# Two sums of weights per unit of seven products, made by GpSimd in place of VectorE

## The chip, the cores and the metric

The kernel runs on one core of one Trainium2 chip. The metric is the device time of one execution in microseconds (us); smaller is better. Five engines work beside each other, each through its own queue of instructions in order: TensorE (PE in the profile, with PEld for its weight loads), VectorE (DVE), ScalarE (ACT), GpSimd (POOL) and SyncE (SP, here only a queue that issues DMAs). An instruction waits in its queue until what it needs is there, and everything behind it in that queue waits too.

## The reference

One layer on 512 tokens of width 1024, all in fp32: a feed-forward block with half weight, a token mixer, a second feed-forward block with half weight, and a last norm.

```python
x = x + 0.5 * swiglu(rmsnorm(x, ffn1_norm), ffn1_w_gate, ffn1_w_up, ffn1_w_down)
x = x + token_mixer(rmsnorm(x, mix_norm), w_in, w_out, ...)
x = x + 0.5 * swiglu(rmsnorm(x, ffn2_norm), ffn2_w_gate, ffn2_w_up, ffn2_w_down)
return rmsnorm(x, final_norm)

def swiglu(x, w_gate, w_up, w_down):
    return (jax.nn.silu(x @ w_gate) * (x @ w_up)) @ w_down
```

The hidden width of a feed-forward block (FFN) is 2816, that is 22 tiles of 128. The change touches only the two FFNs.

## The kernel before

**Precision.** Activations lie transposed, as tiles of 128 features x 512 tokens. Each fp32 operand of a matmul is split into a high half (a copy rounded to the matmul's type fp32r, made by ScalarE) and a low half (what is left, a subtraction by VectorE). Each product is then three matmuls, high x high, high x low and low x high (`mm3`, lines 123 to 125 in the profile). For weights the high half is made in `high` (L391) and the low half in `low` (L395).

**Units of seven products.** The first gate and up tiles of an FFN are plain products. From tile 6 (first FFN) or tile 4 (second) on, the kernel works in units: two by two blocks of weights times two by two blocks of activations, done with seven block products in place of eight (Winograd's form of Strassen's method). A unit `("g", j)` makes the gates of the tiles j and j+1, `("u", j)` their ups, `("d", group, m)` adds a group of eight hidden tiles into the output tiles m and m+1. Plain products `("p", m)`, one for each output tile, stand between them. In order, an FFN has gate and up units, some plain products, four down units (group 0), gate and up units again, more plain products and four down units (group 1); the second FFN ends with half products `l` and `r`. There are 48 units in the two FFNs.

The seven products of a unit are listed in `SEVEN`, each with its block of weights, the PSUM bank it adds into and its block of activations:

```python
SEVEN = (("a11", "w", "b11"), ("s3", "z", "t3"), ("s2", "x", "t2"), ("a12", "w", "b21"),
         ("s1", "y", "t1"), ("a22", "x", "t4"), ("s4", "y", "b22"))
```

Each is 12 matmuls of 256 columns. Two banks are seeded: after product a11 ScalarE copies bank w into bank x (L420), and s2 adds onto it; after s2 it copies x into y, and s1 adds onto it. TensorE can't begin the seeded product before the copy.

**Sums of weights.** Four of the seven blocks of weights are sums. s1 and s3 are made by DMAs in `weight_sums`: SP loads a block into a slot (L346), then a DMA from GpSimd's queue adds a second block onto it (L347, an accumulating DMA, which waits for SP's to land). s2 and s4 are made by VectorE in `total`: s2 = s1 + the left half of the first row of weights (raw0), into a tile of its own (L373); s4 = raw0's right half + s2, in place (L375). So s4 waits until s2's high and low halves are made, and s2 waits for s1. The rows of weights come through `load` (L355) into a pool of three buffers, raw0 and raw1 of a unit in turn; raw1 of a unit therefore takes the buffer that raw0 of the unit before it had, whose last reader on VectorE is s4.

**Order.** Around the units the order on VectorE, ScalarE, SP and GpSimd is written out by a small planner (`pipeline`): every step has a nominal due time, counted from the nominal start of its product (`starts[t]`; STEP is one product of a unit, seven to a unit), and a rank; a heap hands the steps out in order of time, then rank, and each engine gets its instructions in that order. For product t of a unit the steps before the change are:

- `weight_sums`: 14 steps ahead of the unit's first product (two units); later where its slots are still in use by an earlier unit, namely two steps into that unit, and one step later than that rule for one unit of an FFN (`("g", PLAIN + 10)`)
- `load`: 7 steps ahead of the unit
- `total`: 5 steps ahead of product s2 or s4
- `high`: 4 steps ahead; `low`: 3 steps ahead
- `product` itself, and behind it the steps that take its result out of PSUM

The down units share two pairs of slots for s1 and s3 (`GROUP_SUMS`), which the first gate and up unit after group 0 use too, so there the later time applies. After an up unit the casts and subtractions that ready the gates for the down products (`kept`: L547 to L591, with L429 and L432 for the sums of activations) run on ScalarE and VectorE during the unit that follows.

Of the kernel before, what the change touches and what calls it, by code (L numbers as in the profile page):

```python
# [18 lines left out]
ALU = mybir.AluOpType  # L19
# [34 lines left out]
STEP, PLAIN_STEP, HALF_STEP = 1410, 4080, 2130  # L54
# [9 lines left out]
def tile_macaron(ctx: ExitStack, tc, xs, xT, wf, wgu1, wst1, wd1, wdg1, wqk, wv, wo, wgu2, wst2, wd2,  # L64
                 wdg2, lams, relb, onehot, addc, out):
    nc = tc.nc
    V, A, G, T = nc.vector, nc.scalar, nc.gpsimd, nc.tensor
# [136 lines left out]
    def ffn(wgu, wst, wd, wdg, n0, n1, norm, early, res, nm, hooks, ended, first=None,  # L204
# [77 lines left out]
        def up(j):  # L282

            wh, wl = up_w[j]
            pu = ups[j] = pp.tile([P, S], F32, tag="t", name=f"pu{nm}{j}", bufs=2)
            for k in range(KD):
                o = k // 2 * P + k % 2 * 4 * P
                o = slice(o, o + P)
                mm3(pu[:], wh[:, o], wl[:, o], xh[k][:], xl[k][:], k == 0, k == KD - 1)
                yield k  # L290

        def up_weights(j):
            up_w[j] = get_w(wst[j - n1][1], f"su{nm}{j}")
# [18 lines left out]
        ops, begin, starts, now = [], {}, [], 0  # L312
# [14 lines left out]
        def sum_slots(u):  # L327
            if u[0] == "d":
                return GROUP_SUMS[u[2] // 2 % 2]
            if u == units[0]:  # L330
                return PAIR_SLOTS[0][:2]
            if u[1] == PLAIN + 8:
                return GROUP_SUMS[u[0] == "u"]
            o = 2 if u[0] == "g" else 4
            return PAIR_SLOTS[(u[1] - PLAIN) // 2 % 4][o:o + 2]

        sums, raws, second, made, half, g, hs = {}, {}, {}, {}, [], {}, {}
# [29 lines left out]
        def total(t):  # L367

            u, o = ops[t]
            r0 = raws[u][0]  # L370
            if o[0] == "s2":
                s2 = second[u] = tp.tile([P, S], F32, tag="ob", name=f"s2{nm}{t}")[:]
                V.tensor_tensor(s2, sums[u][0][:], r0[:, :512], op=ALU.add)  # L373
            else:
                V.tensor_tensor(second[u], r0[:, 512:], second[u], op=ALU.add)  # L375

        def high(t):
            u, o = ops[t]
# [31 lines left out]
        def at(time, rank, f, *a):  # L410
            count[0] += 1
            heapq.heappush(events, (time, rank, count[0], f, a))
# [4 lines left out]
        def run(until):  # L417
            while events and events[0][0] <= until:
                _, _, _, f, a = heapq.heappop(events)
                f(*a)  # L420
# [210 lines left out]
        def pipeline():  # L631
            seen = {}
            for t, (u, o) in enumerate(ops):
                if o[0] in ("p", "l"):
                    at(starts[t] - 2 * PLAIN_STEP, 1, load, u)
                    at(starts[t] - 3 * STEP, 3, high, t)
                    at(starts[t] - 2 * STEP, 2.5, low, t)
                elif o[0] != "r":
                    if t == begin[u]:
                        if u != units[0]:  # L640

                            time, s0 = starts[t] - 14 * STEP, sum_slots(u)
                            if s0 in seen:
                                time = max(time, starts[begin[seen[s0]] + 2])
                            seen[s0] = u
                            if u == ("g", PLAIN + 10):


                                time += STEP
                            at(time, 1, weight_sums, u)  # L650
                        at(starts[t] - 7 * STEP, 1.5, load, u)
                    if o[0] in ("s2", "s4"):
                        at(starts[t] - 5 * STEP, 2, total, t)
                    at(starts[t] - 4 * STEP, 3, high, t)
                    at(starts[t] - 3 * STEP, 2.5, low, t)
                at(starts[t], 4, product, t)
            if bias is not None:
                at(starts[begin["p", plain]], 5, bias[0])
                at(starts[begin["d", 1, 0] + 2], 5, bias[1])
            up_weights(n1 + 1)  # L660
            for i in range(2):
                for k in up(n1 + i):
                    prepared(n1 + i, k)
                    run((8 * i + k - 15) * 680)
            run(1 << 40)
# [10 lines left out]
        def prepared(j, k):  # L676
            if (j, k) in prepare:
                f, p = prepare[j, k]
                f(p)

        order = ExitStack()
        for j in range(j0, n1):
# [9 lines left out]
            for hf in range(2):  # L692
                wh, wl = get_w(wgu[j, hf], f"gu{nm}{j}_{hf}")
                for kk in range(4):
                    k = hf * 4 + kk
                    for c, pt in ((0, pg), (1, pu)):
                        o = kk * 256 + c * P
# [14 lines left out]
        with order, tc.manual_schedule(engines={mybir.EngineType.DVE, mybir.EngineType.Activation}):  # L712
            pipeline()
# [20 lines left out]
    with tc.manual_schedule(engines={mybir.EngineType.DVE, mybir.EngineType.Activation}):  # L734
        for t in range(4):
            raw = wp.tile([P, 1024], F32, tag="raw", name=f"raw_f{t}")
            h, l = w_place()
            for kk in range(2):
# [18 lines left out]
                for j in range(2):  # L757
                    for c in range(2):
                        o = kk * 512 + (2 * j + c) * P
# [99 lines left out]
    at = {}  # L859
# [611 lines left out]
```

## Time and profile before

| what | value |
|---|---|
| time, median of 3 runs | 936.92 us (936.84 to 937.58) |
| the profiled execution's own time | 937.02 us |
| its span in the trace | 935.3 us |
| TensorE busy | 924.3 us, 99% of the span |
| VectorE busy | 728.5 us, 78% |
| ScalarE busy | 543.4 us, 58% |
| GpSimd busy | 98.2 us, 11% |
| DMA, over the span | 136.71 MB, 146 GB/s |

How to read it: a row of a timeline gives the start in us from the span's start, the duration in us, the engine, the line of the kernel, the operation, and what it writes and reads by the program's names (buffer numbers left out); at the end, in brackets, the idle time of the engine before it and what ended that. A name ends in a or b for the first or second FFN, and g, u, d, p in it stand for the kind of unit: `pxdb` is bank x of a down unit of the second FFN, `s2a` a sum s2 of the first. In a list of waits a row gives the engine, the line waiting, what released it, the time in total, how often, and the longest where that is given. In a view by line, the three numbers behind a count are the shortest, median and longest duration in ns. In the table of windows each row gives the stretch, its length, then the busy time and count of instructions for TensorE, its weight loads, VectorE, ScalarE and GpSimd, the granted clock, the share of the DMA engines and GB/s.

### The profile page before, as it was taken

To read this page: it belongs to the slowest core of one execution; us is meant where nothing else is said; L and a number is where in the kernel's file an instruction comes from. 1 tells how busy PE (TensorE), PEld (TensorE's weight loads), DVE (VectorE), ACT (ScalarE), POOL (GpSimd) and SP (SyncE) were. 2 spreads that over 40 slices of the span, in tenths; PEclk is the share of its full clock that TensorE was granted. 3 is DMA by queue.
4 is the path that set the end of the run, shared out by engine and by line. 5 is a ranking of instruction groups with operands and counts; after the bars stand their busy time and mean duration, and the time that the engine had idled before them with its cause. 6 is when DMAs were issued, how large, how long until landed. Compare 5 with 4: busy or idle time off the path is not lost.

```text
span 935.3 us, 17089 instructions
## 1 busy us (share of the span) xinstructions
PE 924.3 (99%) x6384; PEld 851.0 (91%) x6384; DVE 728.5 (78%) x1504; ACT 543.4 (58%) x1121; POOL 98.2 (11%) x117
## 2 busy tenths in 40 slices
PE   9999999999999999999999999999999999999996
PEld 7888999999999999988978778889999999999996
DVE  6797887677888897678876556797888777888785
ACT  7455664355664575566766664455666455665572
POOL 0001101112202100000000003110111012111000
PEclk9999999999999999999999999999999999999998
DMA  7456646578747562433343213454674677865542
GB/s 251 130 148 147 160 125 173 137 189 220 184 131 203 144 169 91 136 112 113 91 135 91 68 35 129 131 165 106 180 193 116 164 198 193 206 180 152 141 120 91
DMA packets 60372, 136.71 MB, mean 146 GB/s; under 512 B 6832, under 2 KB 9136, under 8 KB 60288
## 3 DMA queue, kind: packets, MB, share of 16 engines
q1 hardware_dynamic: 46288, 110.14, 36.0%
q0 software_dynamic: 14000, 25.47, 17.5%
q8 instruction: 50, 0.82, 0.4%
q14 instruction: 34, 0.28, 0.1%
HBM read 130.30 MB, written 2.14 MB: 142 GB/s over the span
## 4 chain that ended last, share of the span: by engine, by line
PE 94%; DVE 4%; issue 1%; ACT 1%; DMA 1%; SPq 0%; DVEq 0%
PE pv L922 2%; PE pv L921 2%; PE pv L920 2%; PE pwo L123 2%; PE pwo L124 2%; PE pwo L125 2%; PE pua L125 2%; PE pua L124 2%; PE pua L123 2%; PE pq L123 1%; PE pq L124 1%; PE pq L125 1%; PE pk L123 1%; PE pk L125 1%; PE pk L124 1%; PE pda L125 1%
## 5 line engine op out<-in xcount | busy, mean ns | idle before, releaser
L1041 ACT ACTIVATE pr<-pr,mx 128x128 f32<-128x128 f32 (+3 forms) x64 | 36.0, 563 | 35.0 <-DVE mx L1038 34.4
L1038 DVE CUSTOM_DVE_ANT_0 pr<-sc,strip 128x128 f32<-128x128 f32 (+3 forms) x64 | 30.7, 487 | 22.4 <-PE sc L1036 22.1
L391 ACT CAST w<-s2b 128x512 fp32r<-128x512 f32 x50 | 31.0, 620 | 17.1 <-DVE s2b L373 15.6
L395 DVE TENSOR_TENSOR w<-s2b,w 128x512 fp32r<-128x512 f32 x50 | 34.2, 685 | 7.3 <-ACT w L391 7.3
L391 ACT CAST w<-s2a 128x512 fp32r<-128x512 f32 x46 | 28.6, 621 | 18.6 <-DVE s2a L373 15.7
L150 POOL TENSOR_TENSOR sq<-sq,sqt 128x512 f32<-128x512 f32 x7 | 11.0, 1564 | 244.1 <-ACT sqt L149 244.0
L395 DVE TENSOR_TENSOR w<-s2a,w 128x512 fp32r<-128x512 f32 x46 | 31.5, 684 | 6.6 <-ACT w L391 6.5
L920 PE MATMUL pv<-w,xh 128*128 128x256 f32 x128 | 36.2, 283 | 0.0
L921 PE MATMUL pv<-w,xl 128*128 128x256 f32 x128 | 36.2, 283 | 0.0
L922 PE MATMUL pv<-w,xh 128*128 128x256 f32 x128 | 36.2, 283 | 0.0
L123 PE MATMUL pq<-xh,w 128*128 128x512 f32 x64 | 26.2, 410 | 0.0
L123 PE MATMUL pwo<-mh,w 128*128 128x512 f32 x64 | 25.6, 399 | 0.0
L124 PE MATMUL pq<-xl,w 128*128 128x512 f32 x64 | 25.1, 393 | 0.0
L125 PE MATMUL pq<-xh,w 128*128 128x512 f32 x64 | 25.1, 392 | 0.0
L125 PE MATMUL pk<-xh,w 128*128 128x512 f32 x64 | 25.0, 391 | 0.0
L123 PE MATMUL pk<-xh,w 128*128 128x512 f32 x64 | 25.0, 391 | 0.0
L124 PE MATMUL pk<-xl,w 128*128 128x512 f32 x64 | 25.0, 390 | 0.0
L124 PE MATMUL pwo<-ml,w 128*128 128x512 f32 x64 | 25.0, 390 | 0.0
L125 PE MATMUL pwo<-mh,w 128*128 128x512 f32 x64 | 25.0, 390 | 0.0
L921 PEld LDWEIGHTS pv<-w,xl 128*128 128x128 f32 x128 | 24.4, 191 | 0.3
L920 PEld LDWEIGHTS pv<-w,xh 128*128 128x128 f32 x128 | 24.4, 191 | 0.2
L922 PEld LDWEIGHTS pv<-w,xh 128*128 128x128 f32 x128 | 24.5, 191 | 0.0
(691 smaller groups left out, 3992.8 us busy)
## 6 DMA issues: line engine op xcount, KB each, us to landing
raw_qk<-wqk_dram SPq DMA_DIRECT2D x16, 512.0 KB, 3.4
raw0bg<-wst_dram SPq DMA_DIRECT2D x9, 512.0 KB, 4.9
raw_gua<-wgu_dram SPq DMA_DIRECT2D x8, 512.0 KB, 3.4
raw0ag<-wst_dram SPq DMA_DIRECT2D x8, 512.0 KB, 4.5
raw0ad<-wdg_dram SPq DMA_DIRECT2D x8, 512.0 KB, 5.3
strip<-bias_rows SPq DMA_DIRECT2D x16, 256.0 KB, 3.7
raw_v<-wv_dram SPq DMA_DIRECT2D x8, 512.0 KB, 3.3
raw_wo<-wo_dram SPq DMA_DIRECT2D x8, 512.0 KB, 3.3
```

The lines of the kernel that those rows point to most:

```text
L123: T.matmul(po, wh, mh, start=first, stop=False, skip_group_check=on)
L124: T.matmul(po, wh, ml, start=False, stop=False, skip_group_check=on)
L125: T.matmul(po, wl, mh, start=False, stop=last, skip_group_check=on)
L150: G.tensor_tensor(sq[:], sq[:], t[:], op=ALU.add)
L391: A.copy(made[t][0], source(t))
L395: V.tensor_tensor(l, source(t), h.bitcast(F32), op=ALU.subtract)
L920: T.matmul(po, xh[k][:, xs], wh[:, o:o + 256], start=k == 0, stop=False)
L921: T.matmul(po, xl[k][:, xs], wh[:, o:o + 256], start=False, stop=False)
L922: T.matmul(po, xh[k][:, xs], wl[:, o:o + 256], start=False, stop=k == KD - 1)
L1038: V.tensor_tensor_reduce(out=pi, in0=ps[:, :w], in1=st["b"][m][:, w - 1::-1], op0=ALU.add, op1=ALU.min, scale=1.0, scalar=3.0e38, accum_ou ...
L1041: A.activation(pi, pi, AF.Exp, scale=-1.0, bias=st["mx"][:, m, i:i + 1], accum_out=st["ls"][:, m, i:i + 1])
```

## The change

Both adds of `total` go from VectorE's queue (`V`) to GpSimd's (`G`), and their due times move: s2 from 5 steps ahead of its product to 6.5, s4 from 5 to 5.5. The due time sets the place in the order in which GpSimd's queue gets the adds among the accumulating DMAs of `weight_sums`. Nothing else is changed.

```diff
             if o[0] == "s2":
                 s2 = second[u] = tp.tile([P, S], F32, tag="ob", name=f"s2{nm}{t}")[:]
-                V.tensor_tensor(s2, sums[u][0][:], r0[:, :512], op=ALU.add)
+                G.tensor_tensor(s2, sums[u][0][:], r0[:, :512], op=ALU.add)
             else:
-                V.tensor_tensor(second[u], r0[:, 512:], second[u], op=ALU.add)
+                G.tensor_tensor(second[u], r0[:, 512:], second[u], op=ALU.add)
...
                     if o[0] in ("s2", "s4"):
-                        at(starts[t] - 5 * STEP, 2, total, t)
+                        at(starts[t] - (6 if o[0] == "s2" else 5) * STEP - STEP // 2, 2, total, t)
```

## The prediction

> **What bounds the kernel now.** I read the page first, then the list of waits of TensorE's two streams, then the table of windows.
>
> ```profile
> span 935.3 us, 17089 instructions
> ...
> PE 924.3 (99%) x6384; PEld 851.0 (91%) x6384; DVE 728.5 (78%) x1504; ACT 543.4 (58%) x1121; POOL 98.2 (11%) x117
> ```
> ```profile
> PEld pyga L123 <- DVE rbc_n L423: 0.4, 1, 0.4
> ...
> PEld pyda L123 <- DVE x L432: 0.3, 1, 0.3
> ```
> ```profile
> 800.00:820.00 20.00, 20.00 (x171) 20.00 (x171) 17.66 (x34) 12.76 (x27) 3.45 (x4) 1.00 0.85 226
> ```
>
> TensorE is busy for 99% of the span. In all the units of seven products it waited for another engine only where the two rows of the second fence say, 0.7 us together. The window is typical of units that make gates and ups: TensorE full, granted clock 1.00, VectorE 17.66 of 20 us. So work taken off VectorE can win at most those 0.7 us; what counts is whether the change brings TensorE to a stop.
>
> **What moves.** The view by line of the two adds:
>
> ```profile
> L373 DVEq EVENT_SEMAPHORE  x48: 21/21/21, 78.3 to 901.0; - x48
> ...
> L373 DVE TENSOR_TENSOR s2b<-s1bg,raw0bg x9: 679/681/685, 636.2 to 839.3; 128x512 f32<-128x512 f32 x9
> ```
>
> There are 48 units, each with one add for s2 and one for s4: 96 instructions of 0.68 us leave VectorE. In a row each takes 0.60 us of its time (below, 825.31 to 825.91), so VectorE is given 57.6 us. On the path that is worth nothing beyond the 0.7 us. No DMA is added. But GpSimd's queue, until now only descriptors in these stages, gets two waiting adds per unit, and the second load of a unit's rows (raw1) now waits on SP for GpSimd's s4, since it takes the buffer which s4 reads.
>
> **The price of an add on GpSimd** is seen where it adds squares, same shape and type:
>
> ```profile
> 563.56 1.34 POOL L150 TENSOR_TENSOR sq<-sq,sqt 128x512 f32<-128x512 f32 x1 [228.49 <-ACT sqt L149]
> 566.22 3.06 POOL L150 TENSOR_TENSOR sq<-sq,sqt 128x512 f32<-128x512 f32 x2 [1.32 <-ACT sqt L149]
> 572.46 1.29 POOL L150 TENSOR_TENSOR sq<-sq,sqt 128x512 f32<-128x512 f32 x1 [3.17 <-ACT sqt L149]
> 577.48 1.78 POOL L150 TENSOR_TENSOR sq<-sq,sqt 128x512 f32<-128x512 f32 x1 [3.73 <-ACT sqt L149]
> ```
> ```profile
> 564.48 0.69 DVE L1204 TENSOR_TENSOR x<-pwo,x 128x512 f32<-128x512 f32 x1
> ...
> 566.35 1.78 DVE L115 TENSOR_TENSOR w<-raw_wo,w 128x512 fp32r<-128x512 f32 x1
> 568.06 1.77 DVE L137 SCALAR_TENSOR_TENSOR elb<-x,x,ehb 128x512 fp32r<-128x512 f32 x1
> ...
> 577.37 0.74 DVE L137 SCALAR_TENSOR_TENSOR elb<-x,x,ehb 128x512 fp32r<-128x512 f32 x1
> ```
> ```profile
> 565.46 0.62 ACT L149 ACTIVATE sqt<-x 128x512 f32<-128x512 f32 x1
> ```
>
> Undisturbed it takes 1.29 us, and starts 0.14 us after what it waits for (565.46 + 0.62 to 566.22). The two engines exclude each other. VectorE's subtraction at 566.35 took 1.78 instead of 0.68: it went on only at 567.45, 1.23 us after GpSimd's start. GpSimd's add at 577.48 took 0.49 longer, because of VectorE's instruction that ended at 578.11: GpSimd got in 0.14 before that end. Back to back they alternate (GpSimd's pair of 3.06 us, VectorE's 1.78 and 1.77). VectorE's add at 564.48, with one input in PSUM, ran in 0.69 beside GpSimd: only instructions with two SBUF inputs are held. The subtractions that make the low halves (L395) and those on the gates (L429, L547) are of that kind.
>
> [...]
>
> **First term: a gate unit behind a pair** (timelines of VectorE, ScalarE and TensorE):
>
> ```profile
> 822.98 0.68 DVE L395 TENSOR_TENSOR w<-s2b,w 128x512 fp32r<-128x512 f32 x1
> 823.58 0.41 DVE L547 TENSOR_TENSOR h0b<-g0b,h0b 128x256 fp32r<-128x256 f32 x1
> ...
> 824.36 0.42 DVE L429 TENSOR_TENSOR g0b<-g0b 128x256 f32<-128x256 f32 x1
> 824.71 0.68 DVE L395 TENSOR_TENSOR w<-raw0bg,w 128x512 fp32r<-128x512 f32 x1
> 825.31 0.68 DVE L547 TENSOR_TENSOR h2b<-g1b,h1b 128x512 fp32r<-128x512 f32 x1
> 825.91 0.42 DVE L429 TENSOR_TENSOR g0b<-g1b,g0b 128x256 f32<-128x256 f32 x1
> ```
> ```profile
> 826.36 0.62 ACT L577 CAST h3b<-g0b 128x512 fp32r<-128x512 f32 x1 [0.64 <-DVE g0b L429]
> ...
> 827.67 0.38 ACT L420 COPY pygb<-pxgb 128x256 f32<-128x256 f32 x1
> ```
> ```profile
> 827.39 0.28 PE L123 MATMUL pwgb<-xh,w 128*128 128x256 f32 x1
> ...
> 828.81 0.28 PE L123 MATMUL pygb<-txb,w 128*128 128x256 f32 x1
> ```
>
> GpSimd's s4 overwrites s2, so it waits for the low half of s2: 823.66 + 0.14, and then for L547, till 823.85. VectorE's L429 is held to 825.08 and ends at 825.50. GpSimd's next add, s2 of the coming unit, has all it needs; it gets in at 825.36 and holds VectorE to 826.59. So the low half of 824.71 begins at 826.59, 1.88 us late, and so does the second L429 (the add at 826.24, gone from VectorE, stood only behind it). ScalarE's cast h3 waits for that L429, and behind the cast in ScalarE's queue stands the copy that seeds bank y. It now ends at 828.05 + 1.88 = 829.93; TensorE wants it at 828.81. Cover 0.76, stall 1.12 us. Next to be late would be the low half itself: it ends at 827.27, its product begins at 827.39 and reads it third, so that one just holds. The saved VectorE time then brings the up unit back on time. These casts:
>
> ```profile
> ACT h3a L577 <- DVE g0a L429: 9.0, 8, 2.3
> ...
> ACT h3b L577 <- DVE g0b L429: 8.9, 8, 2.3
> ```
>
> Of the 16, four fall into plain products, which have no seeded bank, and one behind the first, single gate; 11 x 1.12 = 12.3 us.
>
> **Second term: GpSimd's queue in the down units.** By the planner's times, the sums of weights (L346, L347) of a unit whose slots are shared are issued two steps into the unit two before it, and s2 of the unit in between two and a half steps into that: behind both accumulating DMAs, which wait for SP's loads to land. On VectorE s2 did not wait for them.
>
> ```profile
> 745.01 0.68 DVE L375 TENSOR_TENSOR s2b<-raw0bd,s2b 128x512 f32<-128x512 f32 x1
> ...
> 749.83 0.68 DVE L373 TENSOR_TENSOR s2b<-s1bd,raw0bd 128x512 f32<-128x512 f32 x1
> ...
> 755.29 0.69 DVE L395 TENSOR_TENSOR w<-s1bd,w 128x512 fp32r<-128x512 f32 x1
> ```
> ```profile
> 752.21 0.85 POOL L347 DMA_DIRECT2D s3bd<-wdg_dram  x1 [1.27 <-DMA s3bd<-wdg_dram]
> 761.51 0.86 POOL L347 DMA_DIRECT2D s1bd<-wdg_dram  x1 [8.45 <-DMA s3bd<-wdg_dram]
> 762.05 1.21 POOL L347 DMA_DIRECT2D s3bd<-wdg_dram  x1
> ```
> ```profile
> 756.00 0.33 SPq L346 DMA_DIRECT2D s1bd<-wdg_dram  x1
> ```
> ```profile
> 750.62 0.62 ACT L391 CAST w<-s2b 128x512 fp32r<-128x512 f32 x1 [1.14 <-DVE s2b L373]
> 751.15 0.61 ACT L391 CAST w<-raw0bd 128x512 fp32r<-128x512 f32 x1
> ...
> 755.17 0.36 ACT L420 COPY pxdb<-pwdb 128x256 f32<-128x256 f32 x1 [2.29 <-PE pwdb L125]
> ```
> ```profile
> 756.39 0.28 PE L123 MATMUL pxdb<-h5b,w 128*128 128x256 f32 x1
> ```
> ```profile
> 766.33 0.28 PE L123 MATMUL pxdb<-h5b,w 128*128 128x256 f32 x1
> ```
>
> A unit lasts 766.33 - 756.39 = 9.94 us. The queue closes a ring: s2 on GpSimd (1.29), its high half on ScalarE (0.11 later, as 749.83 to 750.62; 0.62), its low half (0.68), s4 on GpSimd (0.14, holds VectorE 1.23), two low halves (0.60, 0.68), SP's next load of sums (0.02, as 755.29 to 756.00), to the first accumulate 5.51 (756.00 to 761.51), both out 1.75 (761.51 to 762.05 + 1.21): 12.63 us, 2.69 longer than a unit. Before, the ring was open, since s2 was done at 750.51 without GpSimd.
>
> The first turn starts in the unit of 756.39. There GpSimd is free at 753.06, or 752.46 as the add of 745.01 no longer holds back the low half that SP waits for. s2 ends at 753.75; behind its high half stand two more (0.53 each, 750.62 to 751.15) and then the copy that seeds x: 755.45 to 755.81, in time. One turn on, s2 ends at 766.38 and the copy at 768.44, where TensorE wants 766.33: 2.1 us. The next two lose 2.7 each; the fourth some 2.5, as its sums have slots of their own and SP waits for one low half less. Such a run, 10.0 us, comes in each FFN with the first group of down units and the two units behind; the second group has only two such waits and GpSimd free about a microsecond earlier: I estimate 1 us each. Together 22 us.
>
> **Sum.** 937.0 (profiled, 0.1 above the median) + 12.3 + 22.0 - 0.7 = 970.6 us.
>
> **Rivals.** *Queue alone, 958.3.* VectorE, back to back, may keep GpSimd out until its run ends; then L429 is not late. The pair at 566 to 570 speaks against it, but shows one case. *Exclusion alone, 948.6.* The loads might land sooner when fewer are in flight, closing the gap of 2.69; 5.51 comes from one turn. *Nothing lost, 936.3*: both covers hold (0.76 for the copy to y, 0.58 for the first turn), as GpSimd's s2 runs well ahead in the pairs and VectorE, with 57.6 us less, catches up. It decides if VectorE's delay at L429 stays under 0.76 and a turn under 9.94. This is also the other side: the whole gain would be 0.7 us. *More stops, 994:* all 32 gate and up units lose 1.12, not 11; against it stands the up unit's spare time, for it VectorE idles 2.34 us in the 20 of the window.
>
> **How the numbers follow.** Both terms 0.55 (own range 958 to 984: each term a third smaller or 40% larger), queue alone 0.17, exclusion alone 0.12, nothing lost 0.08, more stops 0.08. The range, 947 to 986, leaves out the last two. Under 0.2% (1.9 us) a measurement of this kernel hardly tells from no change. Slower 0.92; within 0.2% 0.06 and faster 0.02, both from nothing lost.
>
> **What would show it.** GpSimd's busy time should rise by some 96 x 1.3 = 125 us or more, with adds of 1.3 to 1.9 us. VectorE's subtractions beside them should stretch to near 1.8. TensorE should wait for ScalarE's copies (L420) into y in gate units, about 1.1 us, and into x in units around the down groups, 2 to 3 us, three or four in a row, with s2 on GpSimd right behind an accumulate. If TensorE's waits for L420 are missing, or s2 starts before the accumulates, the prediction is wrong.

## The result, and the profile after

The changed kernel takes 968.9 us in the median of four runs (966.57 to 971.77). The kernel before took 937.1 us beside it, so the ratio is 1.034, with an interval of 1.0326 to 1.0353. The prediction said 970.6 us, in a range of 947 to 986. The profiled execution of after took 971.77 us, the longest of the four, with a span of 970.0: against the span before, 34.7 us more. Between the medians the rise is 31.8 us; the account below is of the profiled execution, how the other three divide is not known.

The page of after, with the busy times and, last, the shares of the chain of work that ended last:

```profile
span 970.0 us, 17117 instructions
...
PE 933.7 (96%) x6384; PEld 855.3 (88%) x6384; DVE 738.8 (76%) x1408; ACT 540.4 (56%) x1121; POOL 238.2 (25%) x213
...
PE 74%; DVE 11%; issue 5%; ACT 4%; POOL 3%; DMA 2%; SPq 0%; DVEq 0%; POOLq 0%; ACTq 0%
```

GpSimd's busy time has risen by 140.0 us for 96 adds. VectorE has 96 instructions fewer and yet is busy for 10.3 us more: it stands still inside its instructions (the subtraction at 834.68 below takes 1.77 us, the same one of before at 824.71 took 0.68). TensorE's share of the chain has fallen to 74%. Its list of waits in after (what it waited for: us in total, times, longest):

```profile
PE pyga L123 <- ACT pyga L420: 5.3, 6, 1.2
PE pygb L123 <- ACT pygb L420: 5.2, 6, 0.9
PE pxda L123 <- ACT pxda L420: 3.4, 4, 1.3
...
PE pxub L123 <- ACT pxub L420: 2.8, 1, 2.8
```

These are the two kinds of stop that the prediction named: for the copy that seeds bank y of the gate units (twelve, near 1 us), and for the copy that seeds bank x around the down groups.

**A gate unit of after**, from the timelines of GpSimd, VectorE, ScalarE and TensorE; its first product starts at 832.45:

```profile
833.07 1.40 POOL L375 TENSOR_TENSOR s2b<-raw0bg,s2b 128x512 f32<-128x512 f32 x1 [1.66 <-DVE w L395]
834.43 1.47 POOL L373 TENSOR_TENSOR s2b<-s1bu,raw0bu 128x512 f32<-128x512 f32 x1
```
```profile
833.69 1.06 DVE L429 TENSOR_TENSOR g0b<-g0b 128x256 f32<-128x256 f32 x1
834.68 1.77 DVE L395 TENSOR_TENSOR w<-raw0bg,w 128x512 fp32r<-128x512 f32 x1
...
836.98 0.42 DVE L429 TENSOR_TENSOR g0b<-g1b,g0b 128x256 f32<-128x256 f32 x1
```
```profile
837.42 0.62 ACT L577 CAST h3b<-g0b 128x512 fp32r<-128x512 f32 x1 [2.46 <-DVE g0b L429]
...
838.74 0.37 ACT L420 COPY pygb<-pxgb 128x256 f32<-128x256 f32 x1
```
```profile
839.16 0.38 PE L123 MATMUL pygb<-txb,w 128*128 128x256 f32 x1 [0.87 <-ACT pygb L420]
```

GpSimd stops VectorE twice (L429 takes 1.06 us and L395 1.77, where they took 0.42 and 0.68 before), and VectorE gets one instruction in between (L429 until 834.75). The second L429 starts 4.53 us into the unit. Before it did so at 825.91, 2.78 into the unit of 823.13; it is 1.75 late. Behind it stand the cast of h3 and the copy to y, which ends at 839.11; TensorE waits for it in the last row.

**A turn of the ring in after**: SP's loads, GpSimd and VectorE around a down unit that starts at 784.03.

```profile
778.60 0.33 SPq L346 DMA_DIRECT2D s1bd<-wdg_dram  x1
...
789.78 0.33 SPq L346 DMA_DIRECT2D s1bg<-wst_dram  x1
```
```profile
782.79 0.87 POOL L347 DMA_DIRECT2D s1bd<-wdg_dram  x1 [5.37 <-DVE w L395]
783.37 1.18 POOL L347 DMA_DIRECT2D s3bd<-wdg_dram  x1
783.94 1.93 POOL L373 TENSOR_TENSOR s2b<-s1bd,raw0bd 128x512 f32<-128x512 f32 x1
787.32 1.28 POOL L375 TENSOR_TENSOR s2b<-raw0bd,s2b 128x512 f32<-128x512 f32 x1 [1.46 <-DVE w L395]
```
```profile
786.55 0.69 DVE L395 TENSOR_TENSOR w<-s2b,w 128x512 fp32r<-128x512 f32 x1 [3.32 <-ACT w L391]
...
787.49 1.66 DVE L395 TENSOR_TENSOR w<-raw0bd,w 128x512 fp32r<-128x512 f32 x1
789.07 0.68 DVE L395 TENSOR_TENSOR w<-s1bd,w 128x512 fp32r<-128x512 f32 x1
```

s2 starts right behind the second accumulating DMA, and the next load of s1 waits for the low half that ends at 789.75. One turn, from load to load, is 789.78 - 778.60 = 11.18 us, longer than a unit of 9.94. The eight turns around the first groups of the two FFNs took 11.03 to 12.33 us, 11.5 in the mean.

Comparing the start of every product with its start before gives the loss of each unit, 34.7 us in all. The prediction's eleven gate units are the first two rows. The clock of the last row is told of at the end; the 1.5 us that each of its two falls cost are taken out of the rows above (the eleventh gate unit lost 3.96 in all).

| where | predicted, us | measured, us |
|---|---|---|
| ten gate units behind a pair, copy of y | 11.2 | 11.3 (1.11 to 1.14 each) |
| the eleventh (starts at 242.21) | 1.1 | 2.45 |
| first group of down units and behind, first FFN | 10.0 | 0.74 + 1.24 + 1.76 + 1.75 = 5.5 |
| the same, second FFN | 10.0 | 1.12 + 1.09 + 1.98 + 3.05 = 7.2 |
| second groups | 2.0 | 3.2 + 1.8 = 5.0 |
| gate unit that starts at 93.86, and the gain | -0.7 | 0.8 - 0.5 = 0.3 |
| clock at half rate, twice | 0 | 2.9 |

### The profile page after: what moved, and what is told of

It reads as the page before. It is cut to its first block, busy times and chain, and to the rows that moved or that the text cites. A ratio compares the mean times of both kernels' runs of the same rounds, so it can differ in the third digit from the quotient of the medians.

```text
span 970.0 us, 17117 instructions
## 1 busy us (share of the span) xinstructions
PE 933.7 (96%) x6384; PEld 855.3 (88%) x6384; DVE 738.8 (76%) x1408; ACT 540.4 (56%) x1121; POOL 238.2 (25%) x213
## 4 chain that ended last, share of the span: by engine, by line
PE 74%; DVE 11%; issue 5%; ACT 4%; POOL 3%; DMA 2%; SPq 0%; DVEq 0%; POOLq 0%; ACTq 0%
DVE w L395 4%; ACT w L391 2%; PE pv L922 2%; PE pv L921 2%; PE pv L920 2%; PE pwo L123 2%; PE pwo L124 2%; PE pwo L125 2%; PE pua L124 1%; PE pua L123 1%; PE pua L125 1%; PE pq L123 1%; PE pq L124 1%; PE pq L125 1%; PE pk L123 1%
## 5 line engine op out<-in xcount | busy, mean ns | idle before, releaser
L395 DVE TENSOR_TENSOR w<-s2b,w 128x512 fp32r<-128x512 f32 x50 | 34.2, 684 | 21.1 <-ACT w L391 21.1
L395 DVE TENSOR_TENSOR w<-s2a,w 128x512 fp32r<-128x512 f32 x46 | 31.4, 683 | 15.3 <-ACT w L391 15.3
L347 POOL DMA_DIRECT2D s1ag<-wst_dram x8 | 7.2, 898 | 84.0 <-DMA s3ag<-wst_dram 40.3
L920 PEld LDWEIGHTS pv<-w,xh 128*128 128x128 f32 x128 | 24.4, 191 | 0.2
```

The lines of the kernel that those rows point to most:

```text
L347: nc.gpsimd.dma_start(t[:], b, accum_op=ALU.add)
L395: V.tensor_tensor(l, source(t), h.bitcast(F32), op=ALU.subtract)
L920: T.matmul(po, xh[k][:, xs], wh[:, o:o + 256], start=k == 0, stop=False)
```

## The experiments

**order: the ring alone is opened.** From the changed kernel, the sums of weights come one product later into the unit whose slots they take over, and so stand behind s2 of the next unit in GpSimd's queue:

```diff
-                                time = max(time, starts[begin[seen[s0]] + 2])
+                                time = max(time, starts[begin[seen[s0]] + 3])
...
-                                time += STEP
+                                time += 3 * STEP
```

> The changed kernel, with the sums of weights by DMA handed out one step later where their slots are shared (and three steps later for the one unit that has a step of its own), so that s2 stands ahead of the accumulating DMAs in GpSimd's queue. Theory (two causes: a ring through GpSimd's queue in and behind the down units, and VectorE held at L429 in the gate units): TensorE's waits for the copies into bank x go, the waits for the copies into y stay at some 1.1 us each; 11 x 1.13 = 12.4 us over the kernel before, so 949 to 951. Rival one (the accumulating DMAs themselves are slower because GpSimd is busy, wherever they stand): waits for x stay, 965 to 970. Rival two (VectorE is held in general, order does not matter): 966 to 972.

Measured: 953.4 us (953.1 to 954.8), ratio 1.0173 (1.0156 to 1.019). The waits for x are gone; in TensorE's waits in order those for y remain:

```profile
PE pygb L123 <- ACT pygb L420: 5.6, 6, 1.2
```

So the place of s2 behind the accumulating DMAs makes the ring, and opening it gives back 15.5 us. The regular gate units still lose 1.13 us each. Two others lose 1.86 and 1.67, which is part of why the time is above what was expected.

**copy: the copy of y alone is given more time.** The cast of h3, behind which the copy stood in ScalarE's queue, is handed out a step later, so that it stands behind the copy:

```diff
-            put(n + 2 * STEP, t0_parts)
+            at(n + 3 * STEP, 1, t0_parts)
```

> The changed kernel, with the cast h3 handed out one step later, so that in ScalarE's queue it stands behind the copy that seeds bank y. VectorE and GpSimd exclude each other as before. Theory: the waits for copies into y go (11.3 us, and what the unit with 3.96 us lost that way), the waits for x stay: 955 to 959. Rival (VectorE's lost time itself holds TensorE, through the low halves): little changes, 966 to 970, with TensorE waiting for VectorE's L395 instead of ScalarE's L420.

Measured: 960.7 us (960.1 to 961.4), ratio 1.0248 (1.0233 to 1.0263), somewhat above the 955 to 959 expected. No wait for a copy into y is left, and the regular gate units lose 0.1 us each, ahead of their last product. The waits for x stay, this one first among TensorE's waits in copy:

```profile
PE pxda L123 <- ACT pxda L420: 3.6, 4, 1.2
```

The medians lie 8.2 us apart, the spans 970.0 - 959.4 = 10.6. In the spans the gate units give back 11.6 and one fall of the clock less 1.4, while the waits for x cost 2.4 more than in after.

**both: the two edits together.**

> Both edits together. Theory: the two causes are all there is, so 937 to 940, no faster than the kernel before by more than 0.7 us. If the causes feed each other or a third is there: 943 or more.

Measured: 942.25 us (941.0 to 942.6), ratio 1.0049 (1.0034 to 1.0064). No wait for L420 into x or y is left, so the two terms of the prediction are two separate losses. But the time is 2 to 5 us above what two causes alone should leave: the units still lose 4.7 us, 1.45 and 1.18 of it in two gate units, one in each FFN (the other ten gate units lose 0.12 each, three down units 0.9 together). In the second of these, GpSimd and VectorE of both did this:

```profile
806.44 1.10 POOL L347 DMA_DIRECT2D s3bg<-wst_dram  x1
807.00 1.86 POOL L375 TENSOR_TENSOR s2b<-raw0bg,s2b 128x512 f32<-128x512 f32 x1
808.25 1.85 POOL L373 TENSOR_TENSOR s2b<-s1bu,raw0bu 128x512 f32<-128x512 f32 x1
```
```profile
807.26 3.13 DVE L429 TENSOR_TENSOR g0b<-g0b 128x256 f32<-128x256 f32 x1
```

VectorE did not get in between the two adds; it was held through both. The same stands in after, in the eleventh gate unit of the table:

```profile
243.79 3.75 DVE L395 TENSOR_TENSOR w<-raw0ag,w 128x512 fp32r<-128x512 f32 x1
```

In both cases s4 comes about 0.6 us behind the issue of an accumulating DMA. In the kernel of both, VectorE is held through two adds in four of the 32 pairs that stand back to back, for 3.1 us or more; these are the four with a DMA issue 0.56 us ahead of s4. In the other 28 the last issue lies 0.84 us or more ahead, and none of VectorE's instructions beside them takes longer than 1.8. That is a third cause, tested below.

**s4_only: s2 goes back to VectorE at its old place, s4 stays on GpSimd.**

```diff
-                G.tensor_tensor(s2, sums[u][0][:], r0[:, :512], op=ALU.add)
+                V.tensor_tensor(s2, sums[u][0][:], r0[:, :512], op=ALU.add)
...
-                        at(starts[t] - (6 if o[0] == "s2" else 5) * STEP - STEP // 2, 2, total, t)
+                        at(starts[t] - 5 * STEP - (STEP // 2 if o[0] == "s4" else 0), 2, total, t)
```

> Only s4 on GpSimd, at its place in the changed kernel; s2 on VectorE at its place in the kernel before. Theory: no add on GpSimd stands behind an accumulating DMA that anything near waits for, so no ring; one stop of VectorE in the gate unit makes L429 some 0.7 us late, within the cover of 0.76, so 937 to 939. Rival (each add on GpSimd costs by its exclusion, half as many adds): half of the y waits, 942 to 944.

Measured: 938.7 us (938.2 to 940.3), ratio 1.0017 (1.0008 to 1.0026). Of the waits for L420 into x or y one of 0.3 us is left, in a gate unit that loses 0.7. The one add s4 per unit nearly fits under TensorE, but does not make the kernel faster; it costs 0.7 to 2.4 us.

**s2_only: the other half.** s2 stays on GpSimd at its new place, s4 goes back to VectorE.

```diff
-                G.tensor_tensor(second[u], r0[:, 512:], second[u], op=ALU.add)
+                V.tensor_tensor(second[u], r0[:, 512:], second[u], op=ALU.add)
...
-                        at(starts[t] - (6 if o[0] == "s2" else 5) * STEP - STEP // 2, 2, total, t)
+                        at(starts[t] - 5 * STEP - (STEP + STEP // 2 if o[0] == "s2" else 0), 2, total, t)
```

> The first sum s2 stays on GpSimd at its new place, the second sum s4 goes back to VectorE. Theory (the ring closes through s2 alone, as s2 stands behind the two accumulating DMAs of the next-but-one unit in GpSimd's queue): the ring stays, a turn is about 0.4 us shorter, since s4 costs a VectorE slot of about 0.6 us in place of a stop of 1.2; the waits of TensorE for the copies that seed x (L420) remain, some 15 us instead of 18 to 19. In gate units there is one stop of VectorE per unit, not two: 0 to 0.5 us each for the copy of y. 950 to 957 us. Rival (the ring needs s4 on GpSimd, which follows s2 in the same queue, or the loss of gate units comes from either add): without s4 the x waits go, 937 to 942.

Measured: 960.3 us (958.6 to 961.3), ratio 1.0245 (1.0229 to 1.026). The ring stands with s2 alone: the units around the down groups lose 17.7 us and the gate units 0.5 or less, 0.7 in one. That the loss would get smaller did not come true, and the time is above the 950 to 957 expected. SP's loads and GpSimd in s2_only:

```profile
769.43 0.33 SPq L346 DMA_DIRECT2D s1bd<-wdg_dram  x1
...
780.60 0.33 SPq L346 DMA_DIRECT2D s1bg<-wst_dram  x1
```
```profile
773.64 0.87 POOL L347 DMA_DIRECT2D s1bd<-wdg_dram  x1 [7.75 <-DVE w L395]
774.89 0.85 POOL L347 DMA_DIRECT2D s3bd<-wdg_dram  x1 [0.39 <-issue]
```

This turn is 11.17 us, as the one shown of after. What s4 saves is lost here between the two accumulating DMAs: the second starts 1.25 us behind the first, in after 0.58. In the mean of eight turns it is 11.3 us against 11.5, so 0.2 shorter where 0.4 was expected.

**order_twice: the price of one more stop.** The kernel of order, with the add that makes s2 issued twice (in the runs with added lines the line numbers are one or two higher):

```diff
                 G.tensor_tensor(s2, sums[u][0][:], r0[:, :512], op=ALU.add)
+                G.tensor_tensor(s2, sums[u][0][:], r0[:, :512], op=ALU.add)
```

> The kernel of the run order (no ring), with the add that makes s2 issued twice on GpSimd: the second one writes the same values again, so the output is the same and only GpSimd's and VectorE's time is added. Theory (VectorE is stopped for 1.23 us by each add of GpSimd, and in a gate unit nothing is left to cover it): a third stop ahead of the second L429 costs about 1.15 us more in each of the 11 gate units, L420 waits of about 2.3 instead of 1.2, about 966 us. Rival (VectorE's instruction gets in between the two adds and the low half is what was late, not a count of stops): 953 to 956, as in order.

Measured: 978.9 us (977.3 to 982.1), ratio 1.0451 (1.0428 to 1.0475). GpSimd in one gate unit, then VectorE:

```profile
289.67 1.41 POOL L376 TENSOR_TENSOR s2a<-raw0ag,s2a 128x512 f32<-128x512 f32 x1 [4.99 <-DVE w L396]
291.04 1.46 POOL L373 TENSOR_TENSOR s2a<-s1au,raw0au 128x512 f32<-128x512 f32 x1
292.58 1.62 POOL L374 TENSOR_TENSOR s2a<-s1au,raw0au 128x512 f32<-128x512 f32 x1
```
```profile
291.29 1.77 DVE L396 TENSOR_TENSOR w<-raw0ag,w 128x512 fp32r<-128x512 f32 x1
292.98 1.78 DVE L548 TENSOR_TENSOR h2a<-g1a,h1a 128x512 fp32r<-128x512 f32 x1
```

The engines alternate, and each add costs one stop. In two gate units the loss is 2.23 us, that is 1.10 more than the 1.13 of order, where 1.15 was expected. In seven others it is 3.75: the stop is the same, but behind it TensorE runs at half its clock for a while (granted 0.50 in the windows behind each of the seven), 1.5 us more each. That is 10.6 of the 13 us by which the time is above what was expected.

**dma_ahead and copy_ahead: what keeps VectorE out between two adds.** Both start from the kernel of both. dma_ahead issues a small DMA, of 8 columns to a scratch tensor, directly ahead of each s4. copy_ahead puts a copy of 32 columns there, on GpSimd itself, so that s4 also starts without a wait of its own.

```diff
+                G.dma_start(scratch[:], made[t - 4][1][:, :8].bitcast(F32))
                 G.tensor_tensor(second[u], r0[:, 512:], second[u], op=ALU.add)
```
```diff
+                G.tensor_copy(scratch[:], made[t - 4][1][:, :32].bitcast(F32))
                 G.tensor_tensor(second[u], r0[:, 512:], second[u], op=ALU.add)
```

> The kernel of the run both (the ring opened, the copy of y a step later), with a small DMA (8 columns of the low half of s2 to a scratch tensor in DRAM) issued on GpSimd directly ahead of each s4. Theory (where an add stands directly behind a DMA issue in GpSimd's queue, the next add starts before it has ended, and VectorE is held through both): holds of VectorE of 2.5 to 3.7 us in most gate and up units in place of two of 1.2 to 1.8, and about 1.2 us lost in each gate unit: 953 to 957 us. Rival (the long holds of the two units in both belong to the place, not to the DMA): holds stay at 1.8 or less, and only the 0.6 us of an issue is added: 942 to 945.

> The same as dma_ahead, but what stands directly ahead of each s4 on GpSimd is no DMA: a copy of 32 columns of the same low half to a scratch tile, on the engine itself, so that the wait for VectorE's low half lies on the copy and s4 starts without one. Theory (it is the DMA issue ahead of the two adds that keeps VectorE out of the gap between them): VectorE gets in between s4 and s2 again, holds of 1.8 us or less, 942 to 946 us. Rival (any instruction directly ahead of the pair does it, as s4 then starts without a wait): holds of 3 us in nearly every gate and up unit, as in dma_ahead, 952 to 958.

Measured: dma_ahead 958.4 us (957.5 to 960.6), ratio 1.023 (1.0215 to 1.0245); copy_ahead 943.9 us (943.3 to 944.3), ratio 1.007 (1.0054 to 1.0087). A gate unit of dma_ahead, GpSimd and VectorE:

```profile
840.26 0.57 POOL L376 DMA_DIRECT2D scratchb<-w  x1 [0.25 <-DVE w L397]
840.84 1.31 POOL L377 TENSOR_TENSOR s2b<-raw0bg,s2b 128x512 f32<-128x512 f32 x1
842.10 1.29 POOL L374 TENSOR_TENSOR s2b<-s1bu,raw0bu 128x512 f32<-128x512 f32 x1
```
```profile
840.66 3.02 DVE L431 TENSOR_TENSOR g0b<-g0b 128x256 f32<-128x256 f32 x1
```

The same in copy_ahead:

```profile
256.82 1.29 POOL L377 TENSOR_TENSOR s2a<-raw0ag,s2a 128x512 f32<-128x512 f32 x1
258.07 1.47 POOL L374 TENSOR_TENSOR s2a<-s1au,raw0au 128x512 f32<-128x512 f32 x1
```
```profile
257.16 1.23 DVE L431 TENSOR_TENSOR g0a<-g0a 128x256 f32<-128x256 f32 x1
258.31 1.78 DVE L397 TENSOR_TENSOR w<-raw0ag,w 128x512 fp32r<-128x512 f32 x1
```

With the DMA ahead, VectorE is held for 2.3 us or more in 29 of the 35 back-to-back pairs of dma_ahead (in five of the other six its instruction came too late to be held so long, and in one it got in between), and the regular gate units lose 1.0 us each. (The time is 1.4 us above what was expected; three units of the second down group lose 0.9 to 1.4 us as well.) With a copy ahead VectorE is held through both adds in four of 32 pairs, and in each of these an accumulating DMA had been issued 0.5 to 0.6 us ahead of the copy; in a fifth pair with such an issue (820.56) it got in between. So a DMA issue shortly ahead of the pair is the cause, though it does not act every time. How it keeps VectorE out is not shown.

## Why the prediction was right, and where it was not

- **The bound** (TensorE full, so nothing to win beyond 0.7 us) held. The best of the kernels with an add on GpSimd, s4_only, is at 938.7 us and not below the time before.
- **The price of an add** held: 1.28 us where VectorE leaves it alone (787.32), 1.4 to 1.9 where not; VectorE's subtractions beside it take 1.66 to 1.78 in the rows shown (in after, four beside a single add that starts 0.54 to 0.56 us behind a DMA issue, the first of them at 184.72, take 2.07 to 2.82). That the two alternate held too, except shortly behind a DMA issue (the 3.75 us at 243.79), which the prediction did not see: the one pair on which it rested had none ahead of it. In the eleventh gate unit this made the loss 2.45 us instead of 1.12.
- **First term, 12.3 us.** Place and size were right: 1.11 to 1.14 in ten units against 1.12. VectorE was 1.75 us late, not 1.88. That the sizes agree so well is partly luck: the product begins 1.03 us late (839.16, where 828.81 + 9.32 = 838.13 would be on time), and its matmuls take 0.1 us longer behind the stop (0.38 for the first, where it took 0.28 before), which stands in no step. copy took this term away and left the other.
- **Second term, 22.0 us.** The mechanism was right: the waits come three or four in a row, s2 stands right behind an accumulate, and order takes the term away. Its size was 17.7 us. The turn was put at 12.63; the one shown is 11.18. The step that was mis-sized is the stretch from SP's load to the first accumulate, taken from one turn of before: 5.51 predicted, 782.79 - 778.60 = 4.19 measured. To that comes 1.15 us for the two accumulates where 1.75 was taken, since s2 starts before the second has ended; against it, s2 takes 1.93 and not 1.29. Landing times of the load in before, then in after, from the view of DMA issues (the last number):

```profile
s1bd<-wdg_dram SPq DMA_DIRECT2D x1, 256.0 KB, 4.8
```
```profile
s1bd<-wdg_dram SPq DMA_DIRECT2D x1, 256.0 KB, 3.5
```

  The load itself lands 1.3 us sooner, which is the whole difference. The turn of before was no odd one: the eight loads of s1 around its first groups land after 4.7 to 5.4 us, the eight of after 3.4 to 4.2. The prediction's rival "exclusion alone" rested on this, loads that land sooner with fewer in flight; it came true in half, for the turn stayed 1.24 us above a unit. The windows just ahead of the load in before and in after (the last two numbers are the DMA share and GB/s):

```profile
755.00:756.00 1.00, 1.00 (x11) 1.00 (x10) 0.98 (x2) 0.83 (x2) 0.00 (x0) 1.00 0.40 70
```
```profile
777.00:778.00 1.00, 1.00 (x11) 1.00 (x10) 1.00 (x2) 1.00 (x3) 0.42 (x1) 1.00 0.00 0
```

  In after the load meets DMA engines that stand still. So it is for all eight: in the us ahead of the load their share is 0.40 to 1.12 in before, and 0.00 in after (0.08 once). This speaks for fewer transfers in flight, but no run changed that alone.
- **The second groups** were only estimated, at 2.0 us; they cost 5.0. Some 0.7 of it is no part of the ring: order, which has none, still loses 0.57 and 0.20 in two of these units of the first FFN. Why the rest is over twice the estimate stays open.
- **Half the clock.** 2.9 us came from two falls of the granted clock to 0.50, which stand in no step. So the total came nearer, 34.7 us against 33.6, than its terms, and that is luck: the ring was 4.3 us too large, and the clock (2.9), the held pair (1.3) and the gate unit at 93.86 (0.8) made up for it.
- Of the **rivals**, queue alone (958.3) falls by order, where the gate units go on losing without the ring; exclusion alone (948.6) by copy, where the ring goes on without the stop at y; nothing lost (936.3) by after itself, where VectorE was 1.75 us late against a cover of 0.76 and a turn took 11.18 against 9.94. More stops (994) does not occur: the up units lose nothing for y, as the prediction argued from their spare time. (Its own range, with each term a third smaller, begins at 959 and not 958; nothing rests on that.)

## What to carry to other kernels

When work moves to an engine whose queue also issues DMAs that wait, look first at what it will stand behind in that queue, and whether that closes a ring with the loads it feeds; write out the ring's turn and compare it with the period of the loop. A piece of the turn that is a transfer can't be carried over as it stands: here the share of the DMA engines in the us ahead of the load was 0.40 to 1.12 before and 0.00 to 0.08 after, and the loads landed after 3.4 to 4.2 us where they had taken 4.7 to 5.4. Where two engines hold each other up, count stops per unit on the slower path rather than busy time: here 57.6 us taken off VectorE bought nothing, and two stops per unit made VectorE 1.75 us late, against a cover of 0.76.

## What the runs showed of the hardware that was not expected

**TensorE's granted clock fell to 0.50 behind some stops.** Windows of after around the eleventh gate unit (columns: window, its length, busy time of TensorE, weight loads, VectorE, ScalarE, GpSimd, then the granted clock, the DMA share and GB/s):

```profile
249.00:250.00 1.00, 0.05 (x1) 0.00 (x0) 0.97 (x4) 1.00 (x4) 0.00 (x0) 1.00 0.98 369
...
252.00:253.00 1.00, 1.00 (x7) 1.00 (x7) 0.00 (x0) 0.00 (x0) 0.99 (x2) 0.50 0.85 270
253.00:254.00 1.00, 1.00 (x8) 1.00 (x8) 0.79 (x2) 0.00 (x0) 0.75 (x1) 0.70 0.72 164
254.00:255.00 1.00, 1.00 (x11) 1.00 (x10) 0.95 (x3) 0.65 (x2) 0.00 (x0) 1.00 0.90 147
```

Behind the stop (first row) TensorE is busy throughout, but with 7 matmuls in a us in place of 11. The full rate is back 3.4 us after the first matmul behind the stop (250.24 to 253.61), and some 1.5 us are lost. In the units of seven products this happens twice in after, once in copy, seven times in order_twice and never in before. In every case a stop came just ahead (1.2 and 2.8 us in after, 2.4 in copy, 2.0 in order_twice). But no length of a stop decides it: in order_twice seven of nine equal stops brought it, of 2.0 us each, and in s2_only one of 2.7 us passed with the clock at 1.00 behind it.

```profile
231.00:232.00 1.00, 0.00 (x0) 0.00 (x0) 1.00 (x2) 1.00 (x3) 1.00 (x3) 1.00 0.75 129
232.00:233.00 1.00, 0.00 (x0) 0.00 (x0) 1.00 (x2) 1.00 (x4) 1.00 (x2) 1.00 1.05 147
233.00:234.00 1.00, 0.92 (x7) 0.92 (x8) 1.00 (x2) 0.84 (x3) 0.38 (x1) 1.00 0.86 127
```

Nor did it take one long stop: ahead of 250.24 stood stops of 0.7 and 1.2 us, with 1.4 us of matmuls between them. What decides is open.

**Two adds on GpSimd shortly behind a DMA issue held VectorE as one in most pairs** (29 of 35 in dma_ahead), for 3.02 us in the rows shown of it, where the pair in the rows of copy_ahead, where GpSimd had been idle for 0.93 us ahead of its copy, let VectorE in after 1.23. In the rows of order_twice, where GpSimd had been idle for 4.99 us ahead of its three adds, the two engines alternated, with subtractions of 1.77 and 1.78 us. What makes the difference behind a DMA issue is open.
